# Cross-attention output projection of a hybrid encoder layer: weight units over five raw buffers, loads issued six units ahead, last product held back

## The chip, the cores and the metric

One NeuronCore of a Trainium2 chip runs the whole layer as one program. The metric is the device time in microseconds (us); the kernel before takes 831.02 us, the median of three runs (830.69 to 837.02). A change of about 1%, 8.3 us, can be told from none.

The engines are TensorE (PE in the profile, its weight loads PEld), VectorE (DVE), ScalarE (ACT), GpSimd (POOL) and SyncE (SP). Each works through its own queue of instructions in order. SP and POOL also issue the transfers between DRAM and on-chip memory.

## The reference

One layer of a bidirectional encoder: 512 positions, width 1024, all in float32. Three sub-layers follow each other, each with a norm ahead and a norm behind: a token mixer (attention of two key heads beside a gated scan), cross-attention into 256 memory tokens, and a gated MLP with a convolution of three positions. The change is in the second, and in its way into the third:

```python
def memory_cross_attention(h, m, wq, wkv, wo):
    q = (h @ wq).reshape(b, n, X_HEADS, X_HEAD_DIM)          
    kv = (m @ wkv).reshape(b, nm, 2, X_HEADS, X_HEAD_DIM)
    k, v = kv[:, :, 0], kv[:, :, 1]
    s = jnp.einsum("bqhd,bkhd->bhqk", q, k).astype(jnp.float32) * (X_HEAD_DIM ** -0.5)
    p = jax.nn.softmax(s, axis=-1).astype(v.dtype)
    o = jnp.einsum("bhqk,bkhd->bqhd", p, v).reshape(b, n, X_HEADS * X_HEAD_DIM)
    return o @ wo

x = x + rmsnorm(memory_cross_attention(h, m, w_xq, w_xkv, w_xo), post_x_g)
h = rmsnorm(x, pre_ffn_g)
u = h @ w_up                    # (512, 2 * 2816), then conv, silu(gate) * val, @ w_down
```

## The kernel before

**Products of three.** A float32 operand is split in a high part (rounded to the PE's input type) and a low part (what is left). `mm3` issues three matmuls for each product: high by high, high by low, low by high (L328 to L330 of the kernel before). Activations are split by ACT (the cast, L142) and DVE (the subtraction, L143).

**Weight units.** All weights come as numbered units of 128 x 1024 floats, 512 KB. `load_w` issues a unit's load on SP into a raw buffer (L218), of which the pool `raw` has two. `issue` casts it on ACT (`wh`, L255) and subtracts on DVE (`wl`, L257). `unit` hands the oldest unit to the product that asks for it, and keeps three units issued ahead (`AHEAD`). Units 0 to 57 are the mixer, the memory and the query projection (50 to 57 the queries), 58 to 71 the cross-attention's output projection, then the up-projection, then the down-projection.

**Strassen blocks.** The output projection, the up-projection and the down-projection are products of 2 x 2 blocks with seven products instead of eight. The weight sums that this needs (`t1` to `t4`) are made in DRAM by DMAs: a seed copies one block (SP, behind a load), then an add on POOL's queue accumulates a second block. A few lines set where they go:

```python
SEEDS_AT = frozenset(range(28, 46)) | frozenset(range(58, 72))
ADDS_AT = frozenset(range(42, 50)) | frozenset(range(56, 62))
...
        if i in adds_at and adds:
            with tc.issue_after(nc.gpsimd.tensor_copy(mark, wl[:, 0:1].bitcast(F32)).ins):
                adds.popleft()()
```

A one-column copy on POOL (`mark`, L269) waits until the unit's `wl` is there; the add stands behind it. The adds of the cross sums (`xsum_t`) run in the order t1, t3, t2, t4, two units each; t2 starts from t1's sum and t4 from t2's. The adds for the down-projection (`sum_t`) follow.

**Streams.** Generators are woven by `weave`, which takes a step of the stream that has got least far by its weight. The queries (`queries`, followed by `cross_output`) run beside the heads (`cross`): `scores`, softmax, `turn` (transposes of the probabilities) and `weigh` (probabilities times values). The output projection's products are a11 and d (units 58 to 61), then a22, r2, s1, r4 (64 to 71) and a12 times the kept units 62 and 63, the last product.

**Into the feed-forward.** Evictions of PSUM on DVE end each product: L1180 (`far_near`, behind r2), L1185 (`far_far`, behind s1), L1190 (`near_far`, behind r4), L1208 (behind the last product). `between` then makes the two norms for each block of 128 positions: squares on ACT (L382, L404), small steps on POOL (L353, L356), products on DVE (L384, L389, L360), then four PE transposes per half (L367, `turn_in`), and the split. Blocks 2 and 3 go first, blocks 0 and 1 hang on the last product. The up-projection starts with the right half of the positions (blocks 2 and 3): its first four column blocks use PSUM banks b, s, c and o in 24 matmuls of 256 columns each.

The order of the work comes from a scheduler that places instructions by their dependences and their priority in program order. `issue_after` pins an instruction behind another.

Of the kernel before, what the change touches and what calls it, by code (L numbers as in the profile page):

```python
# [9 lines left out]
F32 = mybir.dt.float32  # L10
# [8 lines left out]
P = 128  # L19
# [9 lines left out]
UP_S = (6, 8, 10, 12, 14, 16, 18)  # L29
N_PLAIN, N_MIX, N_WHOLE = 58, 66, 110 - 2 * len(UP_S)  # L30
N_UP = N_PLAIN + 14
# [9 lines left out]
SIDES_AT = (19, 20)  # L41
LOW_FROM = {"diag": 0, "side": 512}
SEEDS_AT = frozenset(range(28, 46)) | frozenset(range(58, 72))
ADDS_AT = frozenset(range(42, 50)) | frozenset(range(56, 62))
XO_AT = {"w11": 58, "w21": 60, "w12": 62, "w22": 64}
XO_UNITS = ("w11", "w11", "t3", "t3", "keep", "keep", "t4", "t2", "t4", "t2", "t1", "t1", "w22", "w22")
NEG_GROUP = frozenset((p, 1) for p in (2, 5, 6))
# [38 lines left out]
def weave(*streams, late=(), until=None):  # L86
    live = [[g, 0.0, float(total)] for g, total in streams]
    while live:
        live.sort(key=lambda s: s[1] / s[2])
        for i, s in enumerate(live):  # L90
            try:
                step = next(s[0])
            except StopIteration:
                live.remove(s)
                if s[0] is until:
                    return
                break
            if step is None and s[0] in late and i + 1 < len(live):
                s[1] = max(s[1], live[i + 1][1] / live[i + 1][2] * s[2])
            if step is not None:  # L100
                s[1] += step
                clock[0] += step
                stuck[0] = False
                break
        else:
            if stuck[0]:
                raise RuntimeError("no stream can go on")
            stuck[0] = True


def layer(tc, io, out):
# [11 lines left out]
    vp = pool("vp", bufs=1)  # L123
# [5 lines left out]
    def bank(tag):  # L129
        return ps.tile([P, 512], F32, name="ps_" + tag, tag=tag)  # L130

    def big(shape, dt=F32):
        return b8.tile(shape, dt, name="big", tag="big")
# [4 lines left out]
    def tmp4(shape, dt=F32):  # L138
        return t4.tile(shape, dt, name="tmp4", tag="tmp4")
# [13 lines left out]
    pending, last_pow, last_mm = deque(), [None], [None]  # L153
    issued, loaded, taken, last_load, last_low, rooms = [0], [0], [0], [None], [None], [0]
# [3 lines left out]
    def weight_block(name, cols):  # L158
        if name in BLOCKS:
            return io["wd"][BLOCKS.index(name)][:, cols]  # L160
        return sums[name][cols.start // 1024][:, :cols.stop - cols.start]

    def width(u):
        return slice(u * 1024, min(u * 1024 + 1024, NP * 512))

    plan = [("w", i) for i in range(N_PLAIN)]
    for i, name in enumerate(XO_UNITS):
# [2 lines left out]
            plan.append(("keep", XO_AT["w21"] + u))  # L170
        else:
            plan.append(("w", XO_AT[name] + u) if name in XO_AT else ("xs", (name, u)))
    whole, adds_at = N_MIX, set(ADDS_AT)
    for i in range(NF):
        if i in UP_S:
            plan += [(kind, UP_S.index(i)) for kind in ("diag", "side", "sums", "last")]
        else:
            if i >= 2:
                adds_at.update((len(plan), len(plan) + (i - 1 not in UP_S)))
            plan += [("w", whole), ("w", whole + 1)]  # L180
            whole += 2
    assert len(plan) == N_DOWN and whole == N_WHOLE

    spare = [None]

    def raw_room(i):
        if i < N_DOWN:
            rooms[0] += 1
            if rooms[0] % 4 >= 2 and i >= N_UP + 6:
                return tmp4([P, 1024])  # L190
            return rawp.tile([P, 1024], F32, name="raw", tag="raw")
        k = (i - N_DOWN) % 4
        if k < 2:
            return rawp.tile([P, 1024], F32, name="raw", tag="raw")
        if k == 2:
            spare[0] = big([P, 2, 1024])
        return spare[0][:, k - 2, :]

    def source(i):
        kind, n = plan[i]  # L200
        if kind == "xs":
            return cross_sums[n]
        return io["w"][n] if kind in ("w", "keep") else io["wu"][n, ("diag", "side").index(kind)]

    def load_w():
        i = loaded[0]
        loaded[0] += 1
        if i >= N_DOWN:
            p, u = divmod(i - N_DOWN, 6)
            cols = width(u)  # L210
            raw = raw_room(i)[:, :cols.stop - cols.start]
            src = weight_block(PRODUCTS[p][0], cols)
        else:
            if plan[i][0] in ("sums", "last"):
                return None
            raw = raw_room(i)
            src = source(i)
        last_load[0] = nc.sync.dma_start(raw, src).ins  # L218
        return raw
# [15 lines left out]
    raws = deque()  # L235

    def issue():
        i = issued[0]
        issued[0] += 1
        raw = raws.popleft() if raws else load_w()  # L240
        kind = plan[i][0] if i < N_DOWN else "w"
        if kind == "diag" and not raws:
            raws.append(load_w())
        if raw is None:
            raw = pair_sums[kind]
        if kind == "keep":
            kept = big([P, 2, 1024], F32R)
            wh, wl = kept[:, 0], kept[:, 1]
        else:
            wh = wp.tile([P, 1024], F32R, name="wh", tag="wh")  # L250
            wl = wp.tile([P, 1024], F32R, name="wl", tag="wl")
        if raw.shape[1] < 1024:
            wh, wl = wh[:, :raw.shape[1]], wl[:, :raw.shape[1]]
        by_dma = 0 if i in NEG_SCALAR or i in NEG_POOL else LOW_FROM.get(kind, raw.shape[1])
        nc.scalar.copy(wh, raw)  # L255
        if by_dma:
            last_low[0] = nc.vector.tensor_sub(wl[:, :by_dma], raw[:, :by_dma], wh[:, :by_dma].bitcast(F32)).ins  # L257
        if by_dma < raw.shape[1]:
            if i in NEG_POOL:
                nc.gpsimd.tensor_scalar(wl, wh.bitcast(F32), -1.0, 0.0, op0=ALU.mult, op1=ALU.add)  # L260
            else:
                nc.scalar.mul(wl[:, by_dma:], wh[:, by_dma:].bitcast(F32), -1.0)  # L262
            nc.gpsimd.dma_start(wl[:, by_dma:], source(i)[:, by_dma:], accum_op=ALU.add)  # L263
        add_blocks(kind, raw, raws[0] if raws else None)
        pending.append((wh, wl))
        if i in SEEDS_AT:
            seeds.popleft()()
        if i in adds_at and adds:
            with tc.issue_after(nc.gpsimd.tensor_copy(mark, wl[:, 0:1].bitcast(F32)).ins):  # L269
                adds.popleft()()  # L270

    seeds, adds = deque(), deque()

# [36 lines left out]
    def issue_ahead():  # L310
        while issued[0] < min(hold[0], taken[0] + AHEAD):
            issue()
        while N_UP + 4 <= taken[0] and loaded[0] < min(N_UNITS, taken[0] + LOAD_AHEAD[loaded[0] >= N_DOWN]):
            raws.append(load_w())

# [11 lines left out]
    def mm3(o, a, b, start, stop, again=False):  # L327
        nc.tensor.matmul(o, a[0], b[0], start=start, stop=False, skip_group_check=again)  # L328
        nc.tensor.matmul(o, a[0], b[1], start=False, stop=False, skip_group_check=again)  # L329
        last_mm[0] = nc.tensor.matmul(o, a[1], b[0], start=False, stop=stop, skip_group_check=again).ins  # L330

    def blk(b):
        return slice(b * P, (b + 1) * P)
# [151 lines left out]
    def drain(g):  # L485
        for _ in g:
            pass
# [86 lines left out]
    r = rstd_of(rx[:, :NB], NB, D, rx[:, NB:])  # L574
# [42 lines left out]
    v = big([P, NB, T])  # L617
    mix = Act([None] * 4, [None] * 4)

    def pair(act, i):  # L620
        t = big([P, 2, 2, T], F32R)
        act.hi[i], act.lo[i] = t[:, 0], t[:, 1]
# [302 lines left out]
    kT, vv, qT = qkv["kT"], qkv["vv"], qkv["qT"]  # L925
# [159 lines left out]
    def queries():  # L1085
        for c in range(8):
            if c % 2 == 0:
                pair(qx, c // 2)
            yield from proj_fm(hT, T, "b", put_qx(c))
            asked[0] = c + 1  # L1090
        yield from cross_output()
# [74 lines left out]
                weigh((i - 4) // 2)  # L1166
            yield 2.2

    weave((queries(), 58.0), (cross(), 34.0))

    g_post, g_pre = gains("post_x_g", "pre_ffn_g")
    hT = new_act()
# [1 line left out]
    near_y, far_y, kept, last_w = kv["x0"]  # L1174
# [20 lines left out]
    for name, done in (("s1", far_far), ("r4", near_far)):  # L1195
        for i in range(2):
            drain(cross_product(far_y, name, i, unit(2), False, i == 1, True, done if i else None))
    last_y = [bank("b") for _ in range(2)]
    hi, lo = left["a12"]
    for b in range(2):  # L1200
        for i in range(2):
            for k in range(2):
                ac = slice(None), 2 * i + k, blk(b)
                mm3(last_y[b], (hi[ac], lo[ac]), (last_w[i][0][:, k, :], last_w[i][1][:, k, :]),
                    i + k == 0, i + k == 2)
        turns.popleft()()
        c11 = tmp2(tag="tq")
        nc.vector.tensor_add(c11, last_y[b], kept[:, b])  # L1208
        turns.append(second_part(b, got[b], c11, 0))
# [320 lines left out]
```

## Time and profile before

| | |
|---|---|
| time, median of three runs | 831.02 us (830.69 to 837.02) |
| the profiled execution | 832.31 us |
| its span (first to last instruction) | 830.5 us |
| mean granted clock of TensorE | 0.992 |
| PE busy | 804.4 us, 97% |
| DVE, ACT, POOL busy | 603.6, 496.7, 149.0 us |

The page gives the busy time of each engine, then the span in 40 slices of some 21 us, with a digit for tenths of busy time. Places in time are given in us from the start of the span: the query projection's last part lies at 334 to 397 us, the output projection from about 405, the first matmul of the up-projection at 472.5, its steady flow from 491, and the down-projection ends the span. A row of the view of waits has the waiting instruction, what it waited for, the total in us, the number of times and the longest.

### The profile page before, as it was taken

The numbers are of one execution on the slowest core, as the hardware profiler recorded it, in microseconds if no ns is written. First come the engines' busy times: TensorE is split into PE (matmuls) and PEld (weight loads), VectorE is DVE, ScalarE is ACT, GpSimd is POOL, SyncE is SP. The second block draws the span as 40 slices with busy tenths as digits, with TensorE's granted clock in tenths as the row PEclk, the third lists the DMA queues.
The fourth block names the chain that finished last, engine by engine and source line by source line (L and its number), as shares of the span: only waits on it lengthen the run. The fifth ranks groups of instructions, "written<-read, shape, count | busy, mean of one in ns | idle before, by whom it ended". The sixth has DMA issues, their size and how long they took to land.

```text
span 830.5 us, 11785 instructions
## 1 busy us (share of the span) xinstructions
PE 804.4 (97%) x4366; PEld 685.6 (83%) x4366; DVE 603.6 (73%) x915; ACT 496.7 (60%) x820; POOL 149.0 (18%) x229
## 2 busy tenths in 40 slices
PE   9999999999999999999989799999999999999996
PEld 6888878899888878778877498899999998888884
DVE  5467576698896766754585859967777789788765
ACT  5675774678978764545464635645555554566651
POOL 0111211323223113400100322201111111000201
PEclk9999999999999999999999889999999999999999
DMA  7697655779878774757648428666765677368852
GB/s 280 206 264 158 143 136 128 169 192 249 222 197 218 176 231 111 186 185 200 183 145 301 143 78 221 157 149 165 192 170 141 165 190 188 103 196 275 240 126 101
DMA packets 45625, 151.14 MB, mean 182 GB/s; under 512 B 5632, under 2 KB 6912, under 8 KB 45568
## 3 DMA queue, kind: packets, MB, share of 16 engines
q1 hardware_dynamic: 30960, 104.77, 36.6%
q0 software_dynamic: 13312, 42.74, 28.9%
q10 hardware_dynamic: 1296, 2.89, 1.0%
q8 instruction: 34, 0.56, 0.3%
q14 instruction: 23, 0.19, 0.1%
HBM read 146.71 MB, written 33.55 MB: 217 GB/s over the span
## 4 chain that ended last, share of the span: by engine, by line
PE 78%; DVE 7%; ACT 6%; DMA 5%; issue 1%; POOL 1%; SPq 0%; DVEq 0%; POOLq 0%; ACTq 0%
PE ps_b L328 8%; PE ps_b L329 8%; PE ps_b L330 8%; PE ps_s L329 6%; PE ps_s L330 6%; PE ps_s L328 6%; PE ps_o L328 4%; PE ps_o L330 4%; PE ps_o L329 4%; DMA raw<-in_w_dram 4%; PE ps_c L329 4%; PE ps_c L328 4%; PE ps_c L330 4%; PE ps_c L718 2%; ACT wh L255 2%; DVE wl L257 2%
## 5 line engine op out<-in xcount | busy, mean ns | idle before, releaser
L255 ACT CAST wh<-raw 128x1024 fp32r<-128x1024 f32 x112 | 115.7, 1035 | 106.3 <-PE ps_b L329 27.4
L328 PE MATMUL ps_b<-big,wh 128*128 128x512 f32 (+1 forms) x344 | 123.7, 359 | 2.1 <-DVE tmp L1208 1.2
L257 DVE TENSOR_TENSOR wl<-raw,wh 128x1024 fp32r<-128x1024 f32 (+1 forms) x72 | 82.3, 1146 | 56.1 <-ACT wh L255 55.7
L330 PE MATMUL ps_b<-big,wl 128*128 128x512 f32 (+1 forms) x344 | 122.0, 355 | 0.0
L329 PE MATMUL ps_b<-big,wh 128*128 128x512 f32 (+1 forms) x344 | 121.8, 354 | 0.0
L328 PEld LDWEIGHTS ps_b<-big,wh 128*128 128x128 f32 x344 | 66.1, 192 | 11.2 <-DVE big L1081 1.8
L330 PEld LDWEIGHTS ps_b<-big,wl 128*128 128x128 f32 x344 | 66.1, 192 | 9.0 <-DVE wl L257 0.4
L329 PEld LDWEIGHTS ps_b<-big,wh 128*128 128x128 f32 x344 | 66.1, 192 | 8.8 <-DVE big L143 0.7
L329 PE MATMUL ps_s<-wl,big 128*128 128x512 f32 (+1 forms) x148 | 56.9, 385 | 1.7 <-DVE wl L257 1.6
L328 PE MATMUL ps_s<-wh,big 128*128 128x512 f32 (+1 forms) x148 | 56.4, 386 | 0.8 <-ACT wh L255 0.7
L330 PE MATMUL ps_s<-wh,big 128*128 128x512 f32 (+1 forms) x148 | 56.2, 380 | 0.0
L744 DVE TENSOR_TENSOR big<-big 128x512 f32<-128x512 f32 x64 | 48.4, 771 | 9.6 <-ACT tmp L715 5.3
L263 POOL DMA_DIRECT2D wl<-in_w_dram x33 | 29.5, 893 | 117.1 <-ACT wl L262 104.0
L257 DVE TENSOR_TENSOR wl<-tmp,wh 128x1024 fp32r<-128x1024 f32 (+1 forms) x27 | 29.3, 1085 | 26.8 <-ACT wh L255 26.7
L269 POOL COPY mark<-wl 128x1 f32<-128x1 f32 x32 | 8.6, 267 | 209.0 <-DVE wl L257 208.9
L143 DVE TENSOR_TENSOR big<-ps_o,big 128x512 fp32r<-128x512 f32 (+1 forms) x55 | 36.3, 666 | 8.3 <-ACT big L142 8.0
L255 ACT CAST wh<-tmp 128x1024 fp32r<-128x1024 f32 (+1 forms) x27 | 25.3, 937 | 27.9 <-PE ps_b L329 7.4
L328 PE MATMUL ps_c<-big,wh 128*128 128x256 f32 (+1 forms) x120 | 39.3, 328 | 1.7 <-DVE big L143 1.7
L328 PE MATMUL ps_s<-big,wh 128*128 128x256 f32 (+1 forms) x120 | 40.2, 335 | 0.0
L142 ACT CAST big<-ps_o 128x512 fp32r<-128x512 f32 (+1 forms) x55 | 31.5, 575 | 14.4 <-PE ps_o L1113 7.6
L329 PE MATMUL ps_s<-big,wh 128*128 128x256 f32 (+1 forms) x120 | 40.0, 334 | 0.0
L330 PE MATMUL ps_s<-big,wl 128*128 128x256 f32 (+1 forms) x120 | 39.9, 333 | 0.0
(346 smaller groups left out, 2239.6 us busy)
## 6 DMA issues: line engine op xcount, KB each, us to landing
raw<-in_w_dram SPq DMA_DIRECT2D x73, 512.0 KB, 3.4
wl<-in_w_dram POOLq DMA_DIRECT2D x33, 512.0 KB, 6.8
sum_t<-in_wd_dram SPq DMA_DIRECT2D x20, 512.0 KB, 5.9
tmp<-in_w_dram SPq DMA_DIRECT2D x20, 512.0 KB, 4.2
raw<-in_wu_dram SPq DMA_DIRECT2D x14, 512.0 KB, 7.6
sum_t<-in_wd_dram POOLq DMA_DIRECT2D x10, 512.0 KB, 8.2
sum_t<-sum_t POOLq DMA_DIRECT2D x10, 512.0 KB, 8.0
big<-sum_t SPq DMA_DIRECT2D x10, 512.0 KB, 4.6
```

Of the source, the lines that this page charges most:

```text
L142: nc.scalar.copy(hi, src)
L143: (eng or nc.vector).tensor_sub(lo, src, hi.bitcast(F32))
L255: nc.scalar.copy(wh, raw)
L257: last_low[0] = nc.vector.tensor_sub(wl[:, :by_dma], raw[:, :by_dma], wh[:, :by_dma].bitcast(F32)).ins
L263: nc.gpsimd.dma_start(wl[:, by_dma:], source(i)[:, by_dma:], accum_op=ALU.add)
L269: with tc.issue_after(nc.gpsimd.tensor_copy(mark, wl[:, 0:1].bitcast(F32)).ins):
L328: nc.tensor.matmul(o, a[0], b[0], start=start, stop=False, skip_group_check=again)
L329: nc.tensor.matmul(o, a[0], b[1], start=False, stop=False, skip_group_check=again)
L330: last_mm[0] = nc.tensor.matmul(o, a[1], b[0], start=False, stop=stop, skip_group_check=again).ins
L718: nc.tensor.matmul(o[:, b, :], kc[:, blk(b)], qc[:, blk(b)] if m == 1 else pat(qk, b * P, [[2 * m, P // (2 * m)], [T + m, 2], [1, m]]), st ...
L744: nc.vector.tensor_tensor(out=c, in0=c, in1=pat(tt, toff + off, [[2, npair], [gap, 2], [0, m]]), op=ALU.mult)
```

## The change

The adds of the cross sums leave units 42 to 49 and go, two behind one mark, behind units 53 to 56; those of the down-projection go from 56 to 61 to 62 to 67. The loads of units 58 to 71 get five buffers: the two raw ones (`r`), two of the pool that held the values (`v`), and the two halves of one large buffer (`s`, `S`) by turns. From three units ahead of unit 58 on, they are issued up to six units ahead of the unit that is taken. `weave` gets other weights, and the heads are its late stream. The last product's matmuls are pinned behind the last matmul of r4.

```diff
-ADDS_AT = frozenset(range(42, 50)) | frozenset(range(56, 62))
+ADDS_AT = (53, 53, 54, 54, 55, 55, 56, 56) + tuple(range(62, 68))
+XO_AHEAD = 6
+XO_ROOMS = "rrvrrvrsSvrrsS"
...
     def raw_room(i):
+        if N_PLAIN <= i < N_UP and XO_ROOMS[i - N_PLAIN] != "r":
+            room = XO_ROOMS[i - N_PLAIN]
+            if room == "v":
+                return vp.tile([P, 1024], F32, name="ahead", tag="vv")
+            if room == "s":
+                spare[0] = big([P, 2, 1024])
+            return spare[0][:, int(room == "S")]
...
             with tc.issue_after(nc.gpsimd.tensor_copy(mark, wl[:, 0:1].bitcast(F32)).ins):
-                adds.popleft()()
+                for _ in range(min(len(adds), adds_at.count(i))):
+                    adds.popleft()()
...
     def issue_ahead():
         while issued[0] < min(hold[0], taken[0] + AHEAD):
             issue()
+        while N_PLAIN - 3 <= taken[0] < N_UP and loaded[0] < min(N_UP, taken[0] + XO_AHEAD):
+            raws.append(load_w())
...
-    weave((queries(), 58.0), (cross(), 34.0))
+    heads_stream = cross()
+    weave((queries(), 36.0), (heads_stream, 34.0), late=(heads_stream,))
...
     last_y = [bank("b") for _ in range(2)]
+    far_done = last_mm[0]
     hi, lo = left["a12"]
...
-                mm3(last_y[b], (hi[ac], lo[ac]), (last_w[i][0][:, k, :], last_w[i][1][:, k, :]),
-                    i + k == 0, i + k == 2)
+                with tc.issue_after(far_done):
+                    mm3(last_y[b], (hi[ac], lo[ac]), (last_w[i][0][:, k, :], last_w[i][1][:, k, :]),
+                        i + k == 0, i + k == 2)
```

The lines of the changed kernel are some 9 to 15 higher: L257 is L266 there, L367 is L379, L360 is L372, L1180, L1185, L1190 and L1208 are L1193, L1198, L1203 and L1223.

On SP's queue, from the query projection's last loads into the output projection, before (`raw` and `ahead` are buffers of loads, `xsum_t_0` and `xsum_t_1` a sum's two units, `sum_t` the down-projection's sums):

```order
L218 DMA raw<-in_w_dram 128x1024 x13
L281 DMA sum_t_4_3757<-in_wd_dram 128x1024
L218 DMA raw<-in_w_dram 128x1024
L281 DMA sum_t_5_3852<-in_wd_dram 128x512
L218 DMA raw<-xsum_t_0_1885 128x1024
L281 DMA sum_t_0_3889<-in_wd_dram 128x1024
L218 DMA raw<-xsum_t_1_1933 128x1024
```

and now:

```order
L227 DMA raw<-in_w_dram 128x1024 x11
L227 DMA ahead<-xsum_t_0_1885 128x1024
L227 DMA raw<-in_w_dram 128x1024
L291 DMA sum_t_4_3753<-in_wd_dram 128x1024
L227 DMA raw<-in_w_dram 128x1024 x2
L227 DMA raw<-xsum_t_1_1933 128x1024
L291 DMA sum_t_5_3846<-in_wd_dram 128x512
```

The load of unit 60, t3's first, moved ahead of the loads of units 57, 58 and 59.

On DVE, from the last `weigh` to the eviction of s1, before:

```order
L143 TENSOR_TENSOR big<-tmp_3929,big 128x512
L143 TENSOR_TENSOR big<-tmp_3930,big 128x512
L143 TENSOR_TENSOR big<-tmp_4153,big 128x512
L257 TENSOR_TENSOR wl<-raw,wh 128x1024 x3
L1180 TENSOR_TENSOR tmp_4317<-tmp_4317,ps_s 128x512
L257 TENSOR_TENSOR wl<-raw,wh 128x1024
L384 TENSOR_TENSOR tmp_4357<-tmp_4317,big 128x512
L1180 TENSOR_TENSOR tmp_4318<-tmp_4318,ps_s 128x512
L257 TENSOR_TENSOR wl<-raw,wh 128x1024
L384 TENSOR_TENSOR tmp_4369<-tmp_4318,big 128x512
L1185 TENSOR_TENSOR tmp_4405<-ps_s,big 128x512
```

and now:

```order
L145 TENSOR_TENSOR big<-tmp_3922,big 128x512
L266 TENSOR_TENSOR wl<-raw,wh 128x1024 x2
L266 TENSOR_TENSOR wl<-big,wh 128x1024
L1193 TENSOR_TENSOR tmp_4317<-tmp_4317,ps_s 128x512
L1193 TENSOR_TENSOR tmp_4318<-tmp_4318,ps_s 128x512
L266 TENSOR_TENSOR wl<-big,wh 128x1024
L396 TENSOR_TENSOR tmp_4353<-tmp_4317,big 128x512
L396 TENSOR_TENSOR tmp_4365<-tmp_4318,big 128x512
L266 TENSOR_TENSOR wl<-raw,wh 128x1024
L1198 TENSOR_TENSOR tmp_4399<-ps_s,big 128x512
L1198 TENSOR_TENSOR tmp_4423<-ps_s,big 128x512
```

The two blocks' evictions now stand side by side, and the subtractions, one of them from the large buffer, between the pairs.

On PE, at the turn of block 2 (`tmp_4407` before, `tmp_4401` now), from the end of r4 on. Before, with a rest of the last product (`ps_b`) behind it:

```order
L330 MATMUL ps_s<-wh,big 128x512
L367 MATMUL ps_c<-ident,tmp_4407 128x128 x4
L367 MATMUL ps_o<-ident,tmp_4407 128x128 x4
L329 MATMUL ps_b<-big 128x512
L330 MATMUL ps_b<-big 128x512
L328 MATMUL ps_b<-big 128x512
```

and now:

```order
L341 MATMUL ps_b<-big 128x512
L342 MATMUL ps_b<-big 128x512
L379 MATMUL ps_c<-ident,tmp_4401 128x128 x4
L379 MATMUL ps_o<-ident,tmp_4401 128x128 x4
L340 MATMUL ps_b<-big 128x512
```

Before, five matmuls of the last product stood between the turns of blocks 2 and 3, and the other 19 between products ahead of them. Now the 24 stand as twelve ahead of block 2's turn and twelve between the two turns.

More of the change, by code (lines that the diff above doesn't have):

```diff
@@ L172, in layer @@
             plan.append(("w", XO_AT[name] + u) if name in XO_AT else ("xs", (name, u)))
-    whole, adds_at = N_MIX, set(ADDS_AT)
+    whole, adds_at = N_MIX, list(ADDS_AT)
     for i in range(NF):
@@ L178, in layer @@
             if i >= 2:
-                adds_at.update((len(plan), len(plan) + (i - 1 not in UP_S)))
+                adds_at += sorted({len(plan), len(plan) + (i - 1 not in UP_S)})
             plan += [("w", whole), ("w", whole + 1)]
```

## The prediction

> **What bounds the kernel now.** I read the page's busy shares and slices first, then what TensorE waited for, then the stretches around the waits, then the engines inside them.
>
> ```profile
> PE 804.4 (97%) x4366; PEld 685.6 (83%) x4366; DVE 603.6 (73%) x915; ACT 496.7 (60%) x820; POOL 149.0 (18%) x229
> PE   9999999999999999999989799999999999999996
> PEclk9999999999999999999999889999999999999999
> ```
>
> PE is busy 804.4 of 830.5 us, so the number of matmuls sets the time and the change leaves it alone. What can move is the 26 us of idleness and the slices where the granted clock is below 9: both lie at slices 21 to 24, from the cross attention's output projection into the feed-forward (425 to 491 us). The waits of PE there:
>
> ```profile
> PE ps_c L367 <- DVE tmp L360: 3.5, 2, 2.4
> PE ps_c L328 <- DVE big L143: 1.7, 1, 1.7
> PE ps_b L328 <- DVE tmp L1208: 1.2, 1, 1.2
> PE ps_o L328 <- DVE tmp L1147: 1.1, 1, 1.1
> PE ps_s L329 <- DVE wl L257: 1.0, 2, 0.6
> PE ps_o L329 <- DVE big L143: 1.0, 1, 1.0
> PE ps_s L328 <- ACT wh L255: 0.7, 2, 0.4
> PE ps_o L1113 <- DVE tmp L1147: 0.3, 1, 0.3
> ```
>
> Columns: total us, times, longest. They add to 10.5 us. In the query projection (334 to 366 us) the same view has these two from the weight stream, 1.4 us:
>
> ```profile
> PE ps_b L328 <- DVE big L1081: 0.8, 1, 0.8
> PE ps_s L329 <- DVE wl L257: 0.6, 1, 0.6
> ```
>
> The stretches (columns: length, busy PE, PEld, DVE, ACT, POOL with counts, granted clock, DMA share, GB/s):
>
> ```profile
> 425.00:430.00 5.00, 2.60 (x12) 1.57 (x11) 4.74 (x11) 3.71 (x8) 0.00 (x0) 1.00 0.00 0
> 448.00:466.65 18.65, 17.86 (x74) 13.38 (x75) 13.54 (x17) 10.05 (x18) 5.77 (x9) 1.00 0.63 216
> 470.00:476.60 6.60, 2.41 (x11) 1.45 (x11) 6.21 (x10) 4.73 (x10) 0.92 (x3) 0.67 0.48 159
> 476.60:482.30 5.70, 5.68 (x25) 5.39 (x26) 4.88 (x7) 2.69 (x8) 2.48 (x5) 0.50 0.01 4
> 482.30:491.00 8.70, 7.55 (x62) 7.20 (x62) 6.05 (x9) 2.58 (x7) 2.50 (x6) 0.99 0.34 121
> 495.00:800.00 305.00, 305.00 (x1665) 266.34 (x1665) 247.23 (x303) 172.49 (x213) 42.33 (x62) 1.00 0.68 179
> ```
>
> From 470 to 476.6 PE stands and DVE is 94% busy: PE waits for the norms and splits on DVE. At 476.6 PE is full again, but at clock 0.50. After 495 PE has no idle time at all, so whatever is won before it reaches the end whole, if that stretch stays as it is. The chain of waits gives a matmul's step at either clock, and what the weight stream does:
>
> ```profile
> 336.72 9.39 DMA raw<-in_w_dram
> 346.19 1.06 ACT wh L255
> 347.27 1.24 DVE wl L257
> ...
> 361.40 1.24 DVE wl L257
> 362.66 3.39 DMA raw<-in_w_dram
> ...
> 440.62 4.95 DMA raw<-xsum_t
> ...
> 448.51 0.23 PE ps_s L330
> ...
> 478.20 0.21 PE ps_b L329
> ...
> 484.09 0.12 PE ps_s L330
> ```
>
> A load beside the adding DMAs takes 9.39 us, one alone 3.39; cast and subtraction follow, 1.06 and 1.24. With two raw buffers PE runs onto that, at 348 and 363 us and again at 446.
>
> **The change part by part.** It is reckoned against the profiled execution: 832.3 us, a span of 830.5 and 1.8 around it. That is 1.3 above the 831.0 median, which comes off at the end.
>
> *Adds moved.* Eight adding DMAs leave the stretch 307 to 357 us and stand, in pairs, behind units 53 to 56. Their price:
>
> ```profile
> raw<-in_w_dram SPq DMA_DIRECT2D x12, 512.0 KB, 3.3
> xsum_t<-xsum_t POOLq DMA_DIRECT2D x4, 512.0 KB, 8.2
> ```
>
> Without four of them beside units 48 to 52, those loads go from up to 9.39 towards 3.3 us, and both waits of the query projection (1.4 us) go. The loads of units 54 to 59 now share the engines with the pairs. Two buffers at 9.39 + 1.06 + 1.24 = 11.7 us a turn still give a unit each 5.9 us, and a unit holds PE for 24 matmuls at 0.23 = 5.5 us besides the scores: at worst 0.4 us for each of five units, 2. I take 0. In SyncE's queue the load of unit 60 now stands ahead of that of unit 57 and waits for the second pair. The first mark is unit 53's subtraction, at 361.40 before (the row above). At 8.2 us an add, one behind the other, the third add would land 25 us later, at 387, the load 3.4 after it, cast and subtraction done at 393. PE wants unit 57 at about 395: from the subtraction's end at 348.5 half a unit (2.7), seven units (38.5) and some 45 of the scores' steps at 0.12 (5). Free, but with 2 us of cover if the adds go singly; two at a time, as the 9.39 us load suggests, some 15. What it costs without cover is the adds' lateness, one for one. The pairs after it wait for the first ones to land, and their sums are loaded later still. The loads of the gains, which POOL now issues between other adds, are off PE's path.
>
> *Six loads ahead, five buffers.* The wait for `wl` (1.0) and for `wh` (0.7) goes: the 4.95 us load is then issued units before its cast. What is late next is the load into the second `v` room, which waits for the one before it to be subtracted: 0 to 1 us, I take 0.
>
> *Streams.* The last two `weigh` steps, whose 1.1, 1.0 and 0.3 stood bare (425 to 430, PE busy 2.60 of 5), now have the products a11, d, a22 and r2 between them: all 2.4 go. If the scheduler's mixing covers half of it, 1.2 stays.
>
> *Last product held back.* Before, its 24 matmuls fill gaps between 437 and 469, and their results only wait: the first L1208 runs at 475.85. From 448 to 466.65 PE took 74 steps, 17.0 us at 0.23, in 18.65; 0.8 of the loss is shown idle and 0.8 is loss at the changes between fillers and products. That goes. Now the fillers are gone from the hand-overs r2 to s1 and s1 to r4, which share a bank, and stand in two halves of 12 (2.8 us) before the turns of blocks 2 and 3. The rows of DVE:
>
> ```profile
> 462.46 0.68 DVE L1185 TENSOR_TENSOR tmp<-ps_s,big 128x512 f32<-128x512 f32 x1
> ...
> 469.16 0.68 DVE L1190 TENSOR_TENSOR tmp<-ps_s,big 128x512 f32<-128x512 f32 x1
> 470.39 1.42 DVE L360 SCALAR_TENSOR_TENSOR tmp<-big,small 128x512 f32<-128x512 f32 x2 [0.55 <-POOL small L356]
> 471.72 1.22 DVE L257 TENSOR_TENSOR wl<-raw,wh 128x1024 fp32r<-128x1024 f32 x1
> ...
> 475.85 0.68 DVE L1208 TENSOR_TENSOR tmp<-ps_b,big 128x512 f32<-128x512 f32 x1
> 476.45 0.68 DVE L143 TENSOR_TENSOR big<-ps_c,big 128x512 fp32r<-128x512 f32 x1
> ```
>
> - Hand-over r2 to s1: three subtractions of 1.22 now stand ahead of the evictions of r2, 3.7 us, all of it bare in the worst case. The other block's six matmuls and part of the next unit's load cover some: 1.7 (0 to 3.7).
> - Hand-over s1 to r4: at most two, 2.4; I take 0.3.
> - Turns of blocks 2 and 3 (2.4 of the 3.5 us before): from the s1 eviction at 462.46 to the first conv matmul at 474.80 the chain takes 12.3 us. r4 (5.5) and the first half (2.8) cover 8.3 of it to the last split, all of it to the transposes, which come some 4 us sooner. 0 (0 to 4).
> - Start of the conv: from the second transpose of block 3 at 471.95 to the flow at 476.59 it took 4.6 us, with one L257 of 1.22 between; that one now stands earlier, so 3.4. Of the waits 1.7 + 1.2 + 2.4, 5.3 us, this is what is left. With DVE's row as full as before it could be 5.3, with the second half covering it 1.
> - Turns of blocks 0 and 1 (the other 1.1 of L367): they hang on L1223, the eviction of the held product, some 10 us earlier (480.10 before, transposes at 490.06). The conv's two blocks that run meanwhile are 48 matmuls at 0.12, 5.8 us, plus the 3.4 of waiting: 1.0 and 1.8 bare, 2.8 (0 to 4).
>
> ```profile
> 480.10 0.68 DVE L1208 TENSOR_TENSOR tmp<-ps_b,big 128x512 f32<-128x512 f32 x1
> ...
> 490.06 0.63 PE ps_c L367 x4
> ```
>
> *The clock.* In the three stretches above the clock is 0.67, 0.50 and 0.99: half speed for 0.33 x 6.6 / 0.5 + 5.7 + 0.2 = 10.2 us, of which 24 matmuls ran at 0.21 instead of 0.12, 2.3 us. It fell behind waits of 2.4, 1.7 and 1.2 us that nearly touch; it didn't fall at 425 to 430, 2.4 us idle in 5. With one wait of 3.4 left I take it to stay up, narrowly: 2.3 gone (full use of a half-speed interval would cost 5.1).
>
> The Trainium skill ("TensorE: Matmul & The Clock Gate", Part 1) says the clock halves after an idle window of about 3.4 us and is back after about 3.4 us of sustained work. This trace agrees only in part: it halved though no single wait passed 2.4 us, and 5.7 us of dense work went by before it was back. By the page's figure the single wait that I expect would halve it; that is the second rival.
>
> Sum: gone 1.4 + 10.5 + 0.8 + 2.3 = 15.0. New 1.7 + 0.3 + 3.4 + 2.8 = 8.2. Net 6.8, and with the median's 1.3: 832.3 - 6.8 - 1.3 = 824.2, say 824. The new terms at their low ends come to 1.0, which is 817.0; at their high ends, 3.7 + 2.4 + 4 + 5.3 + 4, to 19.4, which is slower than now by 4.
>
> **The rivals.**
> - *All covered* (817 to 820). DVE isn't behind: loads that arrive units early let the casts be done before the evictions come, and the second half of the held product covers the start of the conv. For it: DVE idles in the query stretch. Against: DVE is 94% busy at 470 to 476.6, with the same number of operations to do.
> - *The clock halves again* (827 to 829). The 3.4 us wait sets off another 10.2 us interval, now over dense conv matmuls: 5.1 instead of 0 is 829; with the waits inside it, 827. For it: 3.4 is longer than any wait of before. Against: it is alone.
> - *The wait only moves* (829 to 832). The conv's start still waits 5.3 and blocks 0 and 1 take 4; only the loads' 1.4 + 1.7 are won.
> - *Slower: the chain stands bare* (840). The held product was the cover of the hand-overs, and DVE is in order. If the three and the two subtractions run just ahead of the evictions, 3.7 + 2.4 are bare, the turn of block 2 waits 12.3 - 8.3 = 4.0, the conv start as before, and the clock loses 5.1 more. Won are 1.4, 2.4, 1.7 and 0.8, 6.3. Net 15.2 - 6.3 = 8.9: 840. It decides once the casts of units 68 to 70 start later than r2's last matmul. Against it: with loads six ahead those casts are due some ten microseconds earlier. A rotation of the conv's buffers that has shifted would add to it, but each kind of load keeps a buffer of its own for a round.
>
> **How the numbers follow.** About 1% (8.3 us) can be told from no change: below 822.7 is faster, above 839.3 slower. Forecast as reckoned (821 to 827) 0.50; all covered 0.20; clock again 0.14; only moved 0.08; slower 0.08. Of the forecast's own 0.50 the part under 822.7 is about 0.16. Faster 0.36, slower 0.08, within 0.56. The range 817 to 830 leaves out the slower case, the upper part of "only moved" and the lowest end.
>
> **What would show it.** Right: no PE wait for L266's `wl` at 345 to 365; `weigh`'s L1159 wait gone; the L379 wait for L372 under 1 us at blocks 2 and 3; one wait of about 3 us before the conv's first `ps_b`; granted clock 1.00 in the 10 us behind it; PE without idle after the conv's first units. Wrong: an L340 `ps_s` wait for L1193 or L1198 above 3 us; a clock of 0.5 over full matmuls; a SyncE wait for unit 60's sum that reaches PE near 395; or idle time of PE after 495, where there was none.

## The result, and the profile after

The changed kernel takes 838.60 us, the median of 8 runs (837.06 to 842.23), against 831.01 us for the kernel before in the same series: a ratio of 1.0083 with a 95% interval of 1.0056 to 1.0111. It is slower by 0.8% where the forecast was 824 us, faster by 0.8%; the interval is clear of 1, although the loss is less than the 1% taken above for what can be told from none. The profiled execution, the slowest of the eight, took 842.2 us with a span of 840.4, which is 9.9 us longer than the span before.

The page after, busy shares and slices:

```profile
PE 806.0 (96%) x4366; PEld 691.2 (82%) x4366; DVE 603.3 (72%) x915; ACT 495.6 (59%) x820; POOL 146.8 (17%) x225
PE   8999999999999999997997689999999999999996
PEclk9999999999999999998999789999999999999999
```

PE has as many matmuls as before. The thin slices are no longer 21 to 24 alone: one lies at 380 us, in the query projection, and three between 440 and 504; three of these four have a lower clock. The waits of PE between 334 and 502 us (columns: total us, times, longest):

```profile
PE ps_s L340 <- DVE tmp L1198: 10.7, 1, 10.7
PE ps_b L340 <- DVE big L1093: 5.7, 1, 5.7
PE ps_s L340 <- DVE tmp L1193: 2.0, 1, 2.0
PE ps_c L379 <- DVE tmp L372: 1.1, 1, 1.1
PE ps_s L340 <- ACT big L144: 1.1, 1, 1.1
PE ps_b L340 <- DVE tmp L1223: 0.9, 1, 0.9
```

Nearly all the waits of before are gone: those for `wl` and `wh`, for `weigh`'s L1159, and most of those for the turns. Two new ones stand in their place, 5.7 us before the eviction of a query column (L1093) and 10.7 us before the eviction of s1 (L1198). What stood ahead of those two evictions is in VectorE's timeline (start, duration, and in brackets how long VectorE stood idle before it, and on whom):

```profile
361.02 1.23 DVE L266 TENSOR_TENSOR wl<-raw,wh 128x1024 fp32r<-128x1024 f32 x1 [2.34 <-ACT wh L264]
...
382.29 1.23 DVE L266 TENSOR_TENSOR wl<-raw,wh 128x1024 fp32r<-128x1024 f32 x1 [6.09 <-ACT wh L264]
383.43 0.68 DVE L1093 SCALAR_TENSOR_TENSOR big<-ps_b,big 128x512 fp32r<-128x512 f32 x1
...
467.25 1.23 DVE L266 TENSOR_TENSOR wl<-raw,wh 128x1024 fp32r<-128x1024 f32 x1 [11.43 <-ACT wh L264]
468.39 1.28 DVE L1198 TENSOR_TENSOR tmp<-ps_s,big 128x512 f32<-128x512 f32 x2
```

VectorE wasn't busy. It stood idle for 6.1 and 11.4 us ahead of a weight unit's subtraction, whose cast waited for a load, and the eviction stood behind that subtraction. The units are 57, the last of the queries, and 72, the first of the up-projection. The chain of waits gives their loads:

```profile
371.50 9.57 DMA raw<-in_w_dram
...
448.26 17.81 DMA raw<-in_w_dram
```

Before, a load alone took 3.4 us, and the worst beside an add between 334 and 502 us took 9.39. Unit 57's load was also issued late. SP's timeline, then its waits from 357 to 372 us:

```profile
371.08 0.33 SPq L227 DMA_DIRECT2D ahead<-xsum_t  x1
371.50 0.38 SPq L227 DMA_DIRECT2D raw<-in_w_dram  x1
```

```profile
SPq L227 <- DMA xsum_t<-in_w_dram: 12.0, 1, 12.0
```

The raw buffer for unit 57 was free from 362.3 us on, when the subtraction of unit 55 ended (the row at 361.02). But unit 60's load stands ahead of it in SP's queue, and SyncE waited there 12.0 us for the sum that unit 60 reads. So unit 57's load left 9.2 us late.

What ran beside the 17.81 us load is in the view of the DMA issues between 438 and 467 us (count, size, median us to landing):

```profile
sum_t<-in_wd_dram POOLq DMA_DIRECT2D x4, 512.0 KB, 14.2
sum_t<-in_wd_dram SPq DMA_DIRECT2D x3, 512.0 KB, 16.2
raw<-in_w_dram SPq DMA_DIRECT2D x2, 512.0 KB, 17.8
...
big<-in_pre_ffn_g_dram POOLq DMA_DIRECT2D x1, 512.0 KB, 21.8
```

They are the seeds (SP's queue) and adds (POOL's) of the down-projection's sums, weight loads, and a norm's gain. GpSimd's timeline shows why they came together:

```profile
437.71 0.18 POOL L278 COPY mark<-big 128x1 f32<-128x1 f32 x1 [6.36 <-DVE big L266]
438.20 0.83 POOL L294 DMA_DIRECT2D sum_t<-in_wd_dram  x1 [0.31 <-issue]
438.75 0.47 POOL L278 COPY mark<-wl 128x1 f32<-128x1 f32 x1
438.87 1.12 POOL L294 DMA_DIRECT2D sum_t<-in_wd_dram  x1
...
440.47 1.41 POOL L294 DMA_DIRECT2D sum_t<-in_wd_dram  x1
441.00 1.46 POOL L353 DMA_DIRECT2D big<-in_pre_ffn_g_dram  x1
```

The mark of unit 63 waited 6.4 us for that unit's subtraction (a kept unit, so into a large buffer), which stood on VectorE among `weigh`'s evictions. Behind it four adds and a gain left within 3.3 us. On SP's queue the load of unit 67 waited for the same subtraction, because it goes into the buffer `v` that unit 63 had (there is one such buffer, not two). It left at 437.6, and behind it five seeds and a load by 441.

Behind the waits the granted clock fell again, and more often than before. The stretches (length, PE busy, then the other engines; the clock is the number before the last two):

```profile
378.44:384.17 5.73, 0.01 (x2) 0.01 (x1) 1.83 (x2) 1.54 (x2) 0.81 (x1) 0.95 1.05 315
384.17:390.40 6.23, 6.23 (x23) 5.65 (x24) 1.11 (x1) 1.54 (x2) 0.00 (x0) 0.50 0.66 183
451.12:455.27 4.15, 4.15 (x11) 3.31 (x12) 2.42 (x4) 2.29 (x5) 1.16 (x2) 0.59 1.05 272
458.49:469.22 10.73, 0.00 (x0) 0.03 (x1) 1.97 (x3) 2.20 (x3) 0.00 (x0) 0.67 0.60 175
469.22:472.33 3.11, 3.11 (x7) 2.45 (x8) 2.38 (x4) 1.22 (x4) 1.93 (x3) 0.50 0.54 191
485.99:492.81 6.82, 6.59 (x29) 6.30 (x30) 5.59 (x9) 2.72 (x8) 3.29 (x7) 0.50 0.07 11
502.00:820.00 318.00, 318.00 (x1734) 277.67 (x1733) 253.37 (x310) 177.94 (x221) 42.79 (x63) 1.00 0.67 177
```

At half speed there are 6.8, 3.4, 10.2 and 6.8 us, 27.3 in all against 10.2 before. PE is busy in 19.3 us of it, which costs up to 9.7; before it was 7.3 us and up to 3.7. After 502 PE is full as before.

The account of the 9.9 us: waits between 334 and 502 us are 21.5 us against 13.0 (+8.5), and half speed costs up to 6.0 more. That is 4.6 too much, so as much must be won where no view shows a wait, as between matmuls; the forecast had 0.8 there. That last part is only the remainder of the sum, and no run takes it apart.

### The profile page after: what moved, and what is told of

Same layout as the page of the kernel before. It is cut to its first block, busy times and chain, and to the rows that moved or that the text cites. A ratio compares the mean times of both kernels' runs of the same rounds, so it can differ in the third digit from the quotient of the medians.

```text
span 840.4 us, 11774 instructions
## 1 busy us (share of the span) xinstructions
PE 806.0 (96%) x4366; PEld 691.2 (82%) x4366; DVE 603.3 (72%) x915; ACT 495.6 (59%) x820; POOL 146.8 (17%) x225
## 4 chain that ended last, share of the span: by engine, by line
PE 79%; DMA 7%; ACT 6%; DVE 5%; issue 1%; POOL 1%; SPq 0%; DVEq 0%; POOLq 0%; ACTq 0%
PE ps_b L340 8%; PE ps_b L341 7%; PE ps_b L342 7%; DMA raw<-in_w_dram 7%; PE ps_s L340 6%; PE ps_s L341 6%; PE ps_s L342 6%; PE ps_o L340 5%; PE ps_o L342 5%; PE ps_o L341 5%; PE ps_c L340 4%; PE ps_c L342 4%; PE ps_c L341 4%; PE ps_c L730 2%; ACT wh L264 2%
## 5 line engine op out<-in xcount | busy, mean ns | idle before, releaser
L264 ACT CAST wh<-raw 128x1024 fp32r<-128x1024 f32 (+1 forms) x107 | 110.5, 1034 | 118.4 <-DMA raw<-in_w_dram 42.5
L266 DVE TENSOR_TENSOR wl<-raw,wh 128x1024 fp32r<-128x1024 f32 (+1 forms) x67 | 79.9, 1197 | 70.5 <-ACT wh L264 70.5
L340 PE MATMUL ps_s<-wh,big 128*128 128x512 f32 (+1 forms) x148 | 58.2, 394 | 12.8 <-DVE tmp L1198 10.7
L342 PE MATMUL ps_s<-wh,big 128*128 128x512 f32 (+1 forms) x148 | 57.2, 387 | 0.0
L340 PEld LDWEIGHTS ps_s<-wh,big 128*128 128x128 f32 x148 | 28.5, 193 | 19.0 <-ACT wh L264 11.1
L341 PE MATMUL ps_c<-big,wh 128*128 128x256 f32 (+1 forms) x120 | 39.1, 326 | 0.0
L264 ACT CAST wh<-big 128x1024 fp32r<-128x1024 f32 (+1 forms) x24 | 24.0, 1001 | 25.5 <-PE ps_c L342 5.5
L340 PE MATMUL ps_c<-big,wh 128*128 128x256 f32 (+1 forms) x120 | 39.0, 325 | 0.0
```

## The experiments

Theory A: the adds now come in bunches, loads beside them are late, and a late unit's cast and subtraction stand in their engines' queues ahead of evictions that PE waits for. Theory B: the held product leaves the hand-overs bare. Theory C: the loads' rooms come free late, whatever the adds do.

**e1: the change with the adds of before.**

```diff
-ADDS_AT = (53, 53, 54, 54, 55, 55, 56, 56) + tuple(range(62, 68))
+ADDS_AT = tuple(range(42, 50)) + tuple(range(56, 62))
```

> The changed kernel with the adding DMAs at the units of before (one each at 42 to 49 and 56 to 61). Theory A (bunched DMAs make loads late, and the subtraction of a late unit stands on VectorE ahead of an eviction that TensorE waits for): both long waits of the changed kernel (5.7 us before L1093's eviction at 384, 10.7 us before L1198's at 469) shrink to under 2 us each, the time is 822 to 829 us. Theory B (the held product leaves the hand-over s1 to r4 without cover): the wait before L1198 stays above 5 us, the time is 832 to 838. Theory C (loads issued too late because their rooms come free late, whatever the adds): both waits stay, 836 or more.

Measured 826.50 us against 831.74 of before, 0.993 (0.9904 to 0.9955). PE's waits, 334 to 502 us:

```profile
PE ps_b L340 <- DVE big L1093: 2.1, 1, 2.1
PE ps_s L340 <- DVE tmp L1193: 2.0, 1, 2.0
...
PE ps_s L340 <- DVE tmp L1198: 0.4, 1, 0.4
```

The 10.7 us wait is down to 0.4, and 2.1 are left before L1093 where under 2 was expected. The hold and the rooms are still there, so B and C fall, and A's time came out. One thing more has changed: unit 60's sum is ready early, and its load leaves at 315 us, long before unit 57's. So e1 doesn't tell long loads beside the adds from a stop of SP's queue ahead of that sum.

**e2: the kernel before with the new places of the adds alone.** The loop that issues several adds behind one mark comes with them, and nothing else.

```diff
-ADDS_AT = frozenset(range(42, 50)) | frozenset(range(56, 62))
+ADDS_AT = (53, 53, 54, 54, 55, 55, 56, 56) + tuple(range(62, 68))
```

> The kernel before with nothing but the new places of the adding DMAs (pairs at 53 to 56, then 62 to 67). Theory A: slower than before, with loads of over 9 us beside the pairs and a wait of PE near 365 to 390 of several us; 834 to 842 us. Theories B and C: within 2 us of before, or a gain of the 1.4 us that the loads cost in the query projection, 829 to 832.

Measured 838.99 us against 831.74, 1.0092 (1.0065 to 1.0120). The size is as A expected, the place is not: no wait near 365 to 390, but three waits for `wh`, one of 3.7 us, in the output projection. PE's waits, 334 to 502 us:

```profile
PE ps_s L329 <- ACT wh L255: 6.6, 3, 3.7
PE ps_c L368 <- DVE tmp L361: 4.0, 2, 2.8
```

With two buffers and three units ahead the late units are those that PE needs next, so it waits for the weights themselves. The new places alone make the kernel before as slow as the changed one; in the changed kernel they cost more (1.0083 against the 0.9930 of e1).

That the first wait is absent here speaks for SP's queue. In this kernel unit 57's load stands ahead of unit 60's and leaves as soon as the subtraction of unit 55 has ended:

```profile
361.36 0.33 SPq L218 DMA_DIRECT2D raw<-in_w_dram  x1
```

It takes 10.4 us beside the same pairs, no less than in the changed kernel (9.57), and the column is still evicted 0.3 us before PE needs its bank. So the long loads alone didn't make the wait of 5.7 us; the 9.2 us in SP's queue had to come on top. e2 has the old stream weights too, and no run moved unit 60's load alone.

**e3 and e9: one half of the adds back at a time.** In e3 the cross sums' adds are at 42 to 49 and the others stay at 62 to 67; in e9 the pairs stay at 53 to 56 and the others go to 57 to 62.

```diff
-ADDS_AT = (53, 53, 54, 54, 55, 55, 56, 56) + tuple(range(62, 68))
+ADDS_AT = tuple(range(42, 50)) + tuple(range(62, 68))                     # e3
+ADDS_AT = (53, 53, 54, 54, 55, 55, 56, 56) + tuple(range(57, 63))         # e9
```

> The changed kernel with only the cross sums' adds back at 42 to 49; the down-projection's stay at 62 to 67. Theory A with two separate bunches: the wait at 384 (5.7 us) goes, the wait at 469 (10.7 us) stays; 829 to 833 us. If the first bunch makes the second (because all that follows is late), both go: under 828. Theory C: both stay.

> The changed kernel with its pairs at 53 to 56, but the down-projection's six adds at 57 to 62 instead of 62 to 67: the other half of e3. Theory A, two separate bunches: the wait before L1093 at 384 stays at 4 to 6 us, the wait before L1198 (10.7) falls below 2; 828 to 832 us. If the first bunch, now directly followed by six more adds, grows: the first wait 8 us or more, 833 to 838.

e3 took 837.45 us against 831.74, 1.0073 (1.0050 to 1.0096); e9 took 829.16 against 832.19, 0.9965 (0.9947 to 0.9982). PE's waits in e3 and then in e9, 334 to 502 us:

```profile
PE ps_s L340 <- DVE tmp L1198: 8.8, 1, 8.8
PE ps_s L340 <- DVE tmp L1193: 2.5, 1, 2.5
...
PE ps_b L340 <- DVE big L1093: 1.0, 1, 1.0
```

```profile
PE ps_b L340 <- DVE big L1093: 5.4, 1, 5.4
PE ps_s L340 <- DVE tmp L1193: 3.1, 1, 3.1
...
PE ps_s L340 <- DVE tmp L1198: 0.3, 1, 0.3
```

Each bunch makes its own wait and leaves the other alone. The four cases, by the ratio to before:

| | down-projection's adds at 56 or 57 on | at 62 to 67 |
|---|---|---|
| cross sums' adds singly at 42 to 49 | 0.9930 (e1) | 1.0073 (e3) |
| in pairs at 53 to 56 | 0.9965 (e9) | 1.0083 (the change) |

The move of the six adds of the down-projection costs 1.2 to 1.4%, 10 to 12 us; the move of the eight cross sums' adds costs 0.1 to 0.35%, 1 to 3 us, which the intervals don't tell from nothing. e3 missed its 829 to 833: taking the 5.7 us wait away gave only 1 us. Its profile has small waits in the query stretch again, as before (0.6, 0.8, 1.0 and 1.1 us).

**e10: late, but not in pairs.**

```diff
-ADDS_AT = (53, 53, 54, 54, 55, 55, 56, 56) + tuple(range(62, 68))
+ADDS_AT = tuple(range(50, 58)) + tuple(range(58, 64))
```

> The changed kernel with the cross sums' adds singly at units 50 to 57 and the others at 58 to 63: late, as in the change, but not in pairs. If the pairing is what hurts: no PE wait for L1093 above 2 us, 825 to 829 us. If it is the number of adds in the query stretch, paired or not: a wait of 3 us or more before L1093, 829 to 834.

Measured 828.48 us against 832.19, 0.9953 (0.9936 to 0.9970).

```profile
PE ps_b L340 <- DVE big L1093: 7.2, 4, 2.6
```

The time lies in the range of the first expectation, but the waits fit neither as written: there are four of up to 2.6 us, longer in all than before (7.2 against 5.7). Here unit 57's load isn't held in SP's queue, so adds beside the query loads make waits before the evictions without it and without pairs. But the clock stayed at 1.00 from 356 to 390 us, though PE was idle for 7.2 of 34 us:

```profile
356.00:390.00 34.00, 26.79 (x133) 21.58 (x132) 12.55 (x18) 11.60 (x21) 5.95 (x12) 1.00 0.85 215
```

**e4: the last product not held back, the adds as changed.** The pin is taken off.

```diff
-                with tc.issue_after(far_done):
-                    mm3(last_y[b], ...)
+                mm3(last_y[b], ...)
```

> The changed kernel without the pin that holds the last product's 24 matmuls behind r4. Theory A: the two long waits stay to the size of the time by which the loads are late, less what of the 5.5 us of matmuls the scheduler puts into them; no faster than the changed kernel by more than 3 us, or slower, as the norms lose their cover: 836 to 843 us. Theory B: the wait before L1198 falls by about 5.5 us, 831 to 834 us.

Measured 839.39 us against 831.74, 1.0104 (1.0072 to 1.0135), with the wait before L1198 at 11.8 us and the first at 6.0. The hold isn't what makes them.

**e5: the late unit's cast put behind the eviction.** The loads and adds stay bunched; only ScalarE's and VectorE's queues change. `last_put` holds the two instructions that evict the newest query column.

```diff
-        nc.scalar.copy(wh, raw)
+        with tc.issue_after(last_put[0]) if 57 <= i <= 59 else nullcontext():
+            nc.scalar.copy(wh, raw)
...
-            last_low[0] = nc.vector.tensor_sub(wl[:, :by_dma], raw[:, :by_dma], wh[:, :by_dma].bitcast(F32)).ins
+            with tc.issue_after(last_put[1]) if 57 <= i <= 59 else nullcontext():
+                last_low[0] = nc.vector.tensor_sub(wl[:, :by_dma], raw[:, :by_dma], wh[:, :by_dma].bitcast(F32)).ins
```

> The changed kernel with its bunched adds, but the cast and the subtraction of units 57 to 59 pinned behind the eviction of the query column two units ahead (ScalarE's and VectorE's queues only; no transfer is moved). Theory A, order: TensorE did not lack weights at 384, it lacked a PSUM bank whose eviction stood behind the cast of a late unit that it needed only 11 us later. The 5.7 us wait falls below 1, the loads still take 9 us and more, the half-speed interval behind it goes too; 830 to 834 us. Theory A, bandwidth alone: the wait is only renamed, as a wait of PE for L269's wl or for a later eviction, 4 to 6 us; 837 to 840. In both the wait at 469 stays (10 to 11 us).

Measured 836.75 us against 832.21, 1.0058 (1.0034 to 1.0083). VectorE's timeline, then the stretch of the old wait:

```profile
376.52 0.69 DVE L1096 SCALAR_TENSOR_TENSOR big<-ps_b,big 128x512 fp32r<-128x512 f32 x1 [0.67 <-ACT big L1095]
381.52 1.22 DVE L269 TENSOR_TENSOR wl<-raw,wh 128x1024 fp32r<-128x1024 f32 x1 [4.30 <-ACT wh L266]
...
388.77 1.22 DVE L269 TENSOR_TENSOR wl<-raw,wh 128x1024 fp32r<-128x1024 f32 x1 [5.42 <-ACT wh L266]
395.45 0.69 DVE L1096 SCALAR_TENSOR_TENSOR big<-ps_b,big 128x512 fp32r<-128x512 f32 x1 [0.67 <-ACT big L1095]
```

```profile
378.00:392.00 14.00, 14.00 (x79) 12.18 (x78) 4.56 (x7) 4.21 (x9) 0.81 (x1) 1.00 0.81 231
```

The column's eviction (L1096 here) now runs at 376.5, and PE is full from 378 to 392 at clock 1.00, with the same late loads: it hadn't lacked weights. 3.0 us of wait come back at 396, where the next late unit (its load took 15.8 us) stands on both engines ahead of a softmax and the eviction behind that. So the first wait was made by a late unit standing ahead of an eviction, but a pin at one place moves half of it on; the time falls just short of the second expectation's range and misses the first's, which had the whole wait gone. No run pins unit 72 in the same way; for the second wait the order is read from the timeline.

**e6, e7, e8 and e11: what each other part is worth once the adds are in time.** All have the adds of before. e6 drops the pin, by the diff of e4; e7 puts all rooms to `r` and takes the early loads out; e8 has the old stream weights; e11 drops the pin and the weights, so that the rooms and early loads are the only change to the kernel before.

```diff
-XO_ROOMS = "rrvrrvrsSvrrsS"                                                # e7
+XO_ROOMS = "rrrrrrrrrrrrrr"
-        while N_PLAIN - 3 <= taken[0] < N_UP and loaded[0] < min(N_UP, taken[0] + XO_AHEAD):
-            raws.append(load_w())
...
-    weave((queries(), 36.0), (heads_stream, 34.0), late=(heads_stream,))   # e8, e11
+    weave((queries(), 58.0), (heads_stream, 34.0))
```

> The adds of before, and the last product not held back; beside e1 it prices the hold. If the hold covers the turns of blocks 2 and 3 as reckoned: 1 to 3 us slower than e1 (827.5 to 829.5), with waits for L372 at both turns. If the hold is free of effect once the loads are in time: the same as e1 within 1 us. If it costs cover at the hand-overs: 1 to 2 us faster than e1, and the wait of 2.0 before L1193 gone.

> The adds of before, the loads of units 58 to 71 in the two raw buffers, three units ahead as before; hold and stream weights stay. If the five buffers and the early loads are what gains in e1: 829 to 832 us, with PE waits for L262's wh and L264's wl at 440 to 460 of 2 us or more. If they gain nothing: the same as e1 within 1.5 us.

> The adds of before and the stream weights of before (58 to 34, no late stream); early loads and hold stay. If the streams' new weights cover weigh's waits: 828 to 830 us, with L1159's and L145's waits of 2.4 us back. If not: the same as e1 within 1 us.

> The kernel before with the five buffers and the loads six ahead alone: adds, stream weights and last product as before. From e6, e7 and e8 (the early loads are worth 2.6 us beside the hold, the weights about 0, the hold -1.7): the waits for wh and wl at 440 to 460 gone, 823 to 826 us, a ratio of 0.990 to 0.994 to before. If the early loads pay only together with the held product or the new weights: 828 to 831.

| | us | before | ratio, interval |
|---|---|---|---|
| e1, all but the adds | 826.50 | 831.74 | 0.9930 (0.9904 to 0.9955) |
| e6, and without the hold | 824.82 | 832.21 | 0.9903 (0.9868 to 0.9937) |
| e7, and without the early loads | 829.11 | 832.21 | 0.9962 (0.9943 to 0.9981) |
| e8, and with the old weights | 826.48 | 832.21 | 0.9933 (0.9908 to 0.9958) |
| e11, the early loads alone | 825.87 | 832.19 | 0.9932 (0.9910 to 0.9954) |

The early loads alone give 0.7%, as much as e1, and without them (e7) not quite half of e1's gain goes, with intervals that overlap. But the parts don't add up: the hold and the new weights without the early loads still give 0.4%. The weights move `weigh`'s 2.4 us of waits but not the time: in e8 they are back, and the time is e1's. The hold gives nothing that shows; if anything e6 is faster, but the intervals overlap. The profile of e6 has no wait before L1193 (2.0 in e1), and 7.3 us of waits in all against 10.2.

**e12: e6 with e5's pin on units 54 to 59.**

```diff
-        with tc.issue_after(last_put[0]) if 57 <= i <= 59 else nullcontext():
+        with tc.issue_after(last_put[0]) if 54 <= i <= 59 else nullcontext():
```

> e6 (adds of before, last product not held back) with the casts and subtractions of units 54 to 59 pinned behind the query columns' evictions two units ahead, as in e5. Theory A, order: a late load in the query stretch (up to 9.7 us beside the adds) holds no eviction any more; L1096 waits of PE gone; 821 to 825 us, a ratio of 0.985 to 0.991 to before. If those waits were only chance in single profiles: the same as e6, 824 to 826. If the later casts starve PE: a wait for L269's wl of 1 us or more in the query stretch, 826 or more.

Measured 823.97 us against 833.97, 0.9894 (0.9871 to 0.9916): the lowest time of the kernels here, and 1.1% faster than the kernel before. Of PE's waits, 334 to 502 us:

```profile
PE ps_s L344 <- DVE wl L269: 0.8, 1, 0.8
...
PE ps_b L343 <- DVE big L1096: 0.5, 1, 0.5
```

The wait for `wl` is the 0.8 that e1 has too. A wait of 0.5 us before the evictions is left, where e6 without the pin has 0.2 in its profile. What the pin adds to e6 can't be told from nothing, as the intervals overlap.

## Why the prediction was wrong

- **What failed first: six of the fourteen moved adds weren't costed.** The step on the adds priced the eight of the cross sums and passed over the move of the other six from units 56 to 61 to units 62 to 67: a term put at nothing without a reason. e1 against e3 gives their price, 0.9930 against 1.0073, some 12 us; e9 against the change gives 10. Four of them left together behind unit 63's late mark, and unit 72's load took 17.8 us beside them.
- **The step on the hand-over s1 to r4 (0.3, bounds 0 to 2.4) measured 10.7.** Its mechanism was named, subtractions in VectorE's queue ahead of the evictions. The price counted their durations, 1.22 each, and not what they wait for: one of them waited 11.4 us for a load. With the adds back (e1) the step measured 0.4. The slower rival had the same mechanism at 2.4, and gave 840 us, near the 838.6, by luck: of its 15.2 us only the clock's 5.1 was about right.
- **The cover for the query loads was reckoned for the wrong consumer.** The step saw unit 60's load ahead of unit 57's in SP's queue, asked when PE needs unit 57 (395 us) and found the wait free. The queue did hold that load for 9.2 us, and the unit was still ready by 383.5, in time. But its cast stood ahead of the eviction of a column whose bank PE needed at 378.4. With the cast behind the eviction (e5) PE ran through, and with unit 57's load ahead of unit 60's (e2) there is no such wait. So the sign that the prediction gave for this, a SyncE wait that reaches PE near 395, came by another way, at 378.
- **The clock step failed.** It was to stay up with one wait of 3.4 us. With waits of 5.7, 2.0 and 10.7, and again at the conv's start, it fell four times, 27.3 us at half speed in place of none; in e1, without the long waits, it fell three times, 10.2 us in all. The reading of the trace before was wrong, too: the clock fell at 472.3 us, behind the wait of 2.4 alone, and the waits of 1.7 and 1.2 came after that. On the Trainium skill's "TensorE: Matmul & The Clock Gate" (Part 1, half speed after an idle window of about 3.4 us and full after as much sustained work): the four intervals of 6.8, 3.4, 10.2 and 6.8 us are multiples of 3.4, which agrees. That it fell behind a wait of 2.0 us and not over four waits of 1.1 to 2.6 within 28 us (e10) goes by no length of a single wait, and so not by the page's idle window either; the last section gives what the traces show.
- **Right:** the waits of the query projection for `wl`, of `weigh`, and for the loads at 446 all went. r2 to s1 was 2.0 for 1.7, the turns of blocks 2 and 3 waited 0 for 0, the conv's start 2.1 (1.1 and 0.9) for 3.4, blocks 0 and 1 1.1 for 2.8. PE has no idle stretch after 502. e1 shows the same steps without the long waits: 2.0, 0, 2.7 and 1.1. Its 826.5 us is near the 824 forecast for that reason, but not by every term, as the forecast had no half speed.
- **The loads' step** was right in kind and small in size: 1.7 us of waits were put to it, and e11 gives 5.7 us (3.8 to 7.5) for the early loads alone. Its profiled execution, the slowest of its six, is 2.9 us shorter in span than the one before, with 1.8 us less of waits.
- **Smaller misreadings.** Of the 26 us of idleness some 7 are the end of the span, behind the last matmul, and not at slices 21 to 24. The eight adds stood from 285 to 357 us, not from 307. The half speed before covered 7.3 us of busy PE, up to 3.7 us for the 2.3. The 1.8 us bare at blocks 0 and 1 has no working.

## What to carry to other kernels

A load's price is not only when its own consumer needs it: on an engine that works in order, an instruction that waits for a late transfer holds all that stands behind it, and a far-ahead cast can so hold an eviction that is due now. A queue of loads does the same: a load whose data isn't ready yet holds those behind it. When transfers are moved, count all of them and look at the marks that release them, since one late mark lets a whole string go at once. Here loads issued earlier gained 0.7% alone (e11), and beside the late adds nothing that shows (the change against e2, 1.0083 and 1.0092).

## What was not expected of the hardware

Eleven transfers that left between 438.2 and 445.0 us took 9.5 to 22 us each, and the two loads behind them 17.8 and 17.9, against 3.4 for a load alone and at most 9.4 beside an add between 334 and 502 us before.

Half speed came in intervals of 3.4, 6.8 and 10.2 us (once 13.7, in e4), some of them behind a wait of only 2.0 us (the changed kernel, e1, e5), and stayed away over 7.2 us of idle time in four pieces. In all fourteen traces the changes of the clock lie whole multiples of 3.413 us apart, so a trace can be cut into windows of that length. Three such windows, from before, the changed kernel and e10 (length, PE busy; the clock is the number before the last two):

```profile
468.85:472.26 3.41, 0.97 (x7) 0.76 (x8) 2.86 (x5) 2.48 (x6) 1.63 (x4) 1.00 0.48 163
448.41:451.82 3.41, 1.45 (x7) 0.90 (x6) 3.25 (x4) 0.00 (x0) 0.00 (x0) 1.00 1.06 275
374.94:378.35 3.41, 1.82 (x9) 1.16 (x7) 0.90 (x1) 1.54 (x2) 0.00 (x0) 1.00 0.89 249
```

The first two, with PE idle for 2.4 and 2.0 us, were followed by half speed; the third, with 1.6, was not, since the wait of 2.6 us reached over its edge. Between 20 and 815 us every one of the 29 windows at full speed with more than 1.83 us idle was followed by half speed, and 3 of the 71 with 0.7 to 1.83 us. So it was the idle time in a window, a little over half of it, that went with the fall, and not the length of one wait. No run was made to test this.
